# Loads of keys, values and queries of forgetting attention, issued by SyncE instead of GpSimd

## Chip, cores and metric

The kernel runs on one core of a Trainium2 chip. The metric is the device time of one execution in microseconds. The kernel before took 2594.93 us (median of three runs, 2593.69 to 2598.18).

## What is computed

Two layers of an encoder trunk, 2048 tokens of 1024 columns in float32. Each layer normalizes its input, multiplies it by one input projection, hands the columns to three token mixers (a spatial gate, retention, and forgetting attention, "FoX"), multiplies each branch by a gate, concatenates, applies an output projection, normalizes and adds the input. The change touches the third mixer only:

```python
def _forgetting_attention(q, k, v, f_logit):          # 6 heads of 64 columns
    cum_f = jnp.cumsum(jax.nn.log_sigmoid(f_logit), axis=1)
    for i in range(s // Q_BLOCK):
        logits = jnp.einsum('bqhd,bkhd->bhqk', qb, kb) * scale
        logits = logits + cum_f[:, :, q0:q1, None] - cum_f[:, :, None, :q1]
        logits = jnp.where(causal, logits, -jnp.inf)
        p = jax.nn.softmax(logits, axis=-1)
        outs.append(jnp.einsum('bhqk,bkhd->bqhd', p, vb))
```

## The kernel before

Every float32 product is made exact enough by splitting operands into a high part H and a rest L, both of type float32r, and multiplying HH, HL and LH. A layer runs in this order: the input projection, chunk of columns by chunk, with the mixers' other work in the background; then FoX; then the output projection.

During the input projection the split queries and keys of FoX go to DRAM scratch (`qk`, line 241), the split values too (`vscr`, line 290), and the gates (`gscr`, line 329). FoX reads them back head by head. `FoxLoads` keeps a list of loads: `kv(h)` appends the keys in two halves of 512 KB (64 partitions each) and the values of 1024 KB (rows of 512 bytes), into one of four big buffers; `c(h)` appends two loads of the keys' low part with the cumulated gates (`kL`, 264 KB, 66 partitions); `q(u)` appends two loads for a block of 512 queries (256 KB on 128 partitions, 132 KB on 66). `issue()` takes loads from the list and issues them, since line 567 on GpSimd's queue. The scratch is declared float32, the buffers float32r. A layer has 78 such loads, 156 in all.

The first loads are issued during the last chunk of the input projection (lines 497, 501). After that, `fox()` runs one step per value product. A step holds, in the order "ltesv": the low part of the transposed scores on VectorE (L670), a transpose on TensorE (L659) with its copy on ScalarE (L671), an exponential (L646), up to two score tiles (L612, L613 on TensorE, L630 on VectorE), and a value product (L688 with the high part, L689 with the low part). For some key tiles (`ON_POOL`) the split is done on GpSimd instead: ScalarE copies the transposed tile out (`Ts`, L664), and GpSimd writes the high part (L665) and the low part (L666). Behind each step come one `ld.issue()` and one tick of background work. `ld.kv(h + 1)` is called when the first query block of a head (h > 0) ends, `ld.c(h + 1)` when the second ends.

A finished pair of heads (after each query block of an odd head) goes through `finish()`: the gate is loaded (L714, SyncE), the reciprocal of the row sums is transposed and stored to DRAM (L721, SyncE, 4 KB), read back broadcast over partitions in two loads (L724, SyncE), and GpSimd multiplies gate by reciprocal (L726) and the result by the heads' output (L728); SyncE stores it (L730). Fixed numbers of steps lie between these parts.

The order of the work is the order in which the program is written: every engine takes its instructions in that order, and SyncE and GpSimd take their DMA issues in that order too. An engine, or a queue, that waits for one instruction holds all behind it. A DMA on one of the two queues also waits until the DMA eight before it on that queue has landed.

Of the kernel before, what the change touches and what calls it, by code (L numbers as in the profile page):

```python
# [10 lines left out]
F32 = mybir.dt.float32  # L11
# [4 lines left out]
PSUM = bass.MemoryType.PSUM  # L16
# [8 lines left out]
NSB = 4  # L25
EPS = 1e-6
BIG = 1e30
NU = 29  # 4 KB slots for everything of [128, 1024]
NS = 3  # PSUM banks of the scores
# The pace of the work behind the main stream of matrix products, in its steps.  # L30
LEAD = 19  # FoX: score tiles ahead of the value products
SB = 512  # columns of scores that a second score tile in a step may not pass
PRE = 20  # score tiles during the last chunk of the input projection
EMAX = 2  # exponentials that may wait
TK = (1, 4, 7)  # steps of the last projection tile with a transposed tile
ON_POOL = ((3,), (5,), (4, 8), (4, 8, 12))  # key tiles that GpSimd splits, by query block
ORDER = "ltesv"  # of the parts of a step
FX, RA, RB, RC, RD = 2, 2, 4, 1, 3  # between the parts of a finished head pair
QA = 4  # weight row blocks loaded ahead
OL, OE = 9, 16  # normalized tiles behind the output projection, and the last ones  # L40
OW, OD, OP = 22, 3, 4  # output weights: first step, one not used, one split on VectorE
OPRE = 6  # output projection begun before the end of FoX
WU = 30  # matrix products that bring the tensor engine to its full clock


class Background:
    """Work that follows the main stream of matrix products, some ticks behind."""

    def __init__(self):
        self.active = []  # L50
# [26 lines left out]
def trunk(ctx, tc, a, out):  # L77
    nc = tc.nc
# [7 lines left out]
    tp = ctx.enter_context(tc.tile_pool(name="tp", bufs=2))  # L86
    up = ctx.enter_context(tc.tile_pool(name="up", bufs=NU))
    ctx.enter_context(tc.manual_schedule())
# [4 lines left out]

    BANKS = {"S": (512, NS), "B": (512, 6 - NS), "D": (512, 2)}

# [69 lines left out]
                yield  # L165

    def split(src, on_pool=False):
        """The parts H and L of float32 data, H + L exactly the data, each of 12 bits."""
        t = U("HL", F32R)
        n = 1  # L170
        for d in src.shape[1:]:
            n *= d
        H, L = t[:, 0:n], t[:, 512:512 + n]
        v = (lambda ap: ap) if len(src.shape) == 2 else (lambda ap: ap.rearrange("p (k c) -> p k c", c=src.shape[2]))
        nc.scalar.copy(out=v(H), in_=src)  # L175
        eng = nc.gpsimd if on_pool else nc.vector
        eng.tensor_tensor(out=v(L), in0=src, in1=v(H), op=ALU.subtract)  # L177
        return H, L

    def weight_gen(pieces, dst, pool=lambda k: True, ahead=2):  # L180
        """Loads and splits the eight row blocks of a weight chunk, one per step."""
        pend = []
        for k in range(KT + ahead):
            if k < KT:
                if k % 2 == 0:
                    f2 = U("wf")
                f = f2[:, (k % 2) * 512:(k % 2 + 1) * 512]
                off = 0
                for src, w in pieces:
                    ap = src[k]  # L190
                    o_ = f[:, off:off + w]
                    if len(ap.shape) == 3:
                        o_ = o_.rearrange("p (c e) -> p c e", c=ap.shape[1])
                    nc.sync.dma_start(out=o_, in_=ap)
                    off += w
                pend.append(f[:, :off])
            if k >= ahead:
                dst.append(split(pend[k - ahead], on_pool=pool(k)))
            yield
# [5 lines left out]
        return [token_half(hT, t, g) for g in range(2)]  # L205

    def in_proj(l, hT, w0, cur, next_norm):
        """Input projection and everything of it but FoX attention."""
        w_in = a["w_in"][l].rearrange("(k p) e -> k p e", p=P)
        rz = w_in[:, :, 768:2304].rearrange("k p (c e) -> k p c e", c=4)  # L210
        az = w_in[:, :, 0:768].rearrange("k p (c e) -> k p c e", c=3)
        chunks = [("v", [(w_in[:, :, 3072:3456], 384), (w_in[:, :, 3840:3846], 6)]),
                  ("g", [(w_in[:, :, 3456:3840], 384)]),
                  ("q", [(w_in[:, :, 2304:2688], 384)]), ("k", [(w_in[:, :, 2688:3072], 384)])]
# [1 line left out]
        chunks += [(("r", m), [(rz[:, :, :, m * P:(m + 1) * P], 512)]) for m in range(3)]  # L216
        W = [w0] + [[] for _ in chunks[1:]]

        # rows of a head: L, H, ones of the queries; H, L, cumulative forget gates of the keys
        qk = [[dram.tile([2, 2 * HD + 2, SEQ], F32, name=f"qk{l}{w}{m}") for m in range(3)] for w in range(2)]  # L220
        vscr = dram.tile([SEQ, 6, P], F32, name=f"vscr{l}")
        gscr = [dram.tile([P, SEQ], F32, name=f"gscr{l}{m}") for m in range(3)]
# [3 lines left out]
        qbds = tp.tile([P, 2, 2, P], F32, name="qbds", tag="qbds", bufs=1)  # L226
        nc.vector.memset(qbds, 0.0)

        # ---- queries and keys of FoX, transposed: weights stationary, tokens moving
        def qk_post(which, m, b, z):  # L230
            zt = U("zHL", F32R)
            zH, zL = zt[:, 0:512], zt[:, 512:1024]
# [11 lines left out]
        def T_chunks(hs):  # L244
# [5 lines left out]
            for ci in (1, 2, 3):  # L250
                for b in range(4):
                    nxt = []
                    wg = None
                    for m in range(3):
# [4 lines left out]
                        if m == 0 and b == 3:  # L259
                            wg = weight_gen(chunks[ci + 1][1], W[ci + 1], lambda k: k % 3 > 0, QA)  # L260
                            for _ in range(QA):
                                next(wg)
# [17 lines left out]
                    hs = nxt  # L280
            return hs

        # ---- the other chunks: tokens stationary, weights moving
        def v_post(t, z):
            vv = up.tile([P, 6, 2, HD], F32R, name="vv", tag="u")
            zv = heads(z[:, 0:384])
# [184 lines left out]
        for ci in (0, 4, 5, 6, 7, 8):  # L471
# [3 lines left out]
            last = ci == len(chunks) - 1  # L475
            if ci == 4:
                cur = T_chunks(cur)
            for t in range(NT):
# [6 lines left out]
                for k in range(KT):  # L485
                    H, L = cur[k // 4]
# [10 lines left out]
                    if last and k % 4 == 3:  # L497
                        loads.issue()
                    if fx and k % 2 and fx.chunks < PRE and t >= 10:
                        fx.s_step()  # L500
                        loads.issue()
                        fx.e_step()
                    if last and t == NT - 1 and k in TK:
                        fx.l_step()
# [20 lines left out]
    class FoxLoads:  # L525
# [38 lines left out]
        def issue(self, n=1):  # L564
            for _ in range(min(n, len(self.queue))):
                o, i = self.queue.pop(0)
                nc.gpsimd.dma_start(out=o, in_=i)

    class Fox:
        """FoX attention in steps: score steps (one 128 x <=512 tile) run ahead of value steps."""  # L570

        def __init__(self, loads, gscr, y):
            self.ld, self.gscr, self.y = loads, gscr, y
# [74 lines left out]
        def t_step(self):  # L648
# [12 lines left out]
            PH, PL = t[:, 0:512], t[:, 512:1024]  # L661
            if j in ON_POOL[s] and (h, s) != (5, 3):
                Ts = U("Ts")
# [68 lines left out]
    def fox(fx):  # L732
        ld = fx.ld
        for i, (h, s, j) in enumerate(fx.V):
            for op in ORDER:
                if op == "e":
                    fx.e_step()
                    if len(fx.exps) > EMAX:
                        fx.e_step()
                elif op == "l":  # L740
                    fx.l_step()
                elif op == "s":
                    n = 0
                    while n < 2 and fx.si < len(fx.S) and fx.cols < fx.vcols + LEAD * 512 - n * SB:
                        fx.s_step()
# [27 lines left out]
    def out_proj(l, y, W, og, x_src, x_dst, hT, next_w, ahead):  # L773
# [31 lines left out]
                yield from norm(o, pre, hT, t, OL if t < NT - 2 else OE, "B")  # L805

        def last_tile(cur):
            """The last token tile, its first half of columns ahead of the other."""
            t = NT - 1
            x = load_x(x_src(t))  # L810
            o = U("o")
            junk = U("junk")
            ss = small("ss", [P, 2])
            rs = small("rs", [P, 1])
            cs = [slice(g * 512, (g + 1) * 512) for g in range(2)]
            for g in range(2):
                oo = bank("oo", "S")
                for k in range(KT):
                    H, L = cur[k // 4]
                    c = slice((k % 4) * P, (k % 4 + 1) * P)  # L820
                    w = W[2 * k + g]
                    for xx, i, first, last in ((H, 0, True, False), (H, 1, False, False), (L, 0, False, True)):
                        mm(oo, lhsT=xx[:, c], rhs=w[i], start=(k == 0 and first), stop=(k == KT - 1 and last))  # L823
                    bg.tick()
                nc.scalar.activation(out=junk[:, cs[g]], in_=oo, func=AF.Square, accum_out=ss[:, g:g + 1])  # L825
                nc.vector.tensor_tensor(out=o[:, cs[g]], in0=oo, in1=post[:, cs[g]], op=ALU.mult)
            nc.gpsimd.tensor_tensor(out=rs, in0=ss[:, 0:1], in1=ss[:, 1:2], op=ALU.add)  # L827
            nc.gpsimd.tensor_scalar(out=rs, in0=rs, scalar1=1.0 / DM, scalar2=EPS, op0=ALU.mult, op1=ALU.add)  # L828
            nc.gpsimd.tensor_tensor(out=rs, in0=rs, in1=mhalf[:, 0:1], op=ALU.pow)
            for c in cs:  # L830
                nc.vector.scalar_tensor_tensor(out=o[:, c], in0=o[:, c], scalar=rs, in1=x[:, c], op0=ALU.mult, op1=ALU.add)  # L831
                nc.sync.dma_start(out=x_dst(t)[:, c], in_=o[:, c])
# [14 lines left out]
        for t in range(NT):  # L847
# [9 lines left out]
            for k in range(KT):  # L857
                H, L = cur[k // 4]
# [18 lines left out]
        if hT is None:  # L877
            last_tile(cur)
# [26 lines left out]

    wg = weight_gen(first_w(0), W0, lambda k: k % 3 > 0)
    xq[0] = load_x(x_src(0))
    for _ in range(WU):  # the tensor engine at its full clock when the first tile is ready
        nc.tensor.transpose(bank("warm", "B")[:, 0:P], ident, ident)
    pg = load_gain(a["pre_gain"][0])  # L910
    next(wg)
# [2 lines left out]
    first = norm(xq.pop(0), pg, hT, 0, 1, "B", (slice(0, 512), slice(512, DM)))  # L914
# [77 lines left out]
```

## Time and profile before

| | |
|---|---|
| median of three runs | 2594.93 us |
| span of the profiled execution | 2588.5 us |
| TensorE (PE) busy | 2522.0 us, 97% |
| VectorE (DVE) busy | 1663.9 us, 64% |
| ScalarE (ACT) busy | 1258.1 us, 49% |
| GpSimd (POOL) busy | 943.0 us, 36% |
| moved by the hardware-described DMA queue (SyncE's) | 176.61 MB |
| moved by the software-described DMA queue (GpSimd's) | 50.74 MB |

The span runs from the first to the last instruction of the profiled execution; the median of the runs is 6.4 us above it. The profile tells for each instruction when it started, how long it took, and, where its engine sat idle before it, what ended that idle time. A wait is put down to the event that came last. FoX runs from about 749 to 1115 us in the first layer and from about 2030 to 2397 us in the second.

### The profile page before, as it was taken

To read this page: it belongs to the slowest core of one execution; us is meant where nothing else is said; L and a number is where in the kernel's file an instruction comes from. 1 tells how busy PE (TensorE), PEld (TensorE's weight loads), DVE (VectorE), ACT (ScalarE), POOL (GpSimd) and SP (SyncE) were. 2 spreads that over 40 slices of the span, in tenths; PEclk is the share of its full clock that TensorE was granted. 3 is DMA by queue.
4 is the path that set the end of the run, shared out by engine and by line. 5 is a ranking of instruction groups with operands and counts; after the bars stand their busy time and mean duration, and the time that the engine had idled before them with its cause. 6 is when DMAs were issued, how large, how long until landed. Compare 5 with 4: busy or idle time off the path is not lost. (4 is left out here: it accounts for less than half of the span.)

```text
span 2588.5 us, 39556 instructions
## 1 busy us (share of the span) xinstructions
PE 2522.0 (97%) x13112; PEld 2149.4 (83%) x13112; DVE 1663.9 (64%) x4173; ACT 1258.1 (49%) x2967; POOL 943.0 (36%) x1528
## 2 busy tenths in 40 slices
PE   9999999999999999999999999999999999999998
PEld 8888899787888777778898889987878887777887
DVE  5544577666668888854454445666676788878433
ACT  7543433333336788843344444333332478768221
POOL 3111366444443444431120114664344435353200
PEclk9999999999999999999999999999999999989999
DMA  6435411101051556254431354101012415653443
GB/s 212 115 88 121 112 38 37 41 14 37 12 106 39 111 100 130 76 183 134 135 126 69 100 120 101 49 22 38 22 30 42 81 38 128 109 110 97 166 146 114
DMA packets 188428, 229.87 MB, mean 89 GB/s; under 512 B 24640, under 2 KB 130048, under 8 KB 186688
## 3 DMA queue, kind: packets, MB, share of 16 engines
q1 hardware_dynamic: 147712, 176.61, 23.7%
q0 software_dynamic: 40512, 50.74, 10.7%
q8 instruction: 104, 1.70, 0.3%
q14 instruction: 100, 0.82, 0.1%
HBM read 149.20 MB, written 78.09 MB: 88 GB/s over the span
## 5 line engine op out<-in xcount | busy, mean ns | idle before, releaser
L489 PE MATMUL z<-HL 128*128 128x512 f32 (+2 forms) x1536 | 588.5, 383 | 1.8 <-ACT HL L175 1.8
L491 PE MATMUL z<-HL 128*128 128x512 f32 (+2 forms) x1536 | 561.3, 365 | 3.7 <-DVE HL L177 3.6
L490 PE MATMUL z<-HL 128*128 128x512 f32 (+2 forms) x1536 | 559.1, 364 | 0.6 <-POOL HL L177 0.6
L177 DVE TENSOR_TENSOR HL<-hT,HL 128x512 fp32r<-128x512 f32 x576 | 420.7, 779 | 42.1 <-ACT HL L175 33.6
L865 PE MATMUL oo<-HL 128*128 128x512 f32 x1488 | 355.4, 395 | 0.2
L177 POOL TENSOR_TENSOR HL<-wf,HL 128x512 fp32r<-128x512 f32 (+2 forms) x150 | 179.0, 1199 | 451.2 <-ACT HL L175 332.8
L175 ACT CAST HL<-hT 128x512 fp32r<-128x512 f32 x576 | 324.0, 625 | 0.0
L865 PEld LDWEIGHTS oo<-HL 128*128 128x128 f32 x1488 | 273.3, 188 | 57.8 <-DVE HL L177 1.1
L491 PEld LDWEIGHTS z<-HL 128*128 128x128 f32 x1536 | 288.6, 188 | 38.6 <-DVE HL L177 5.3
L489 PEld LDWEIGHTS z<-HL 128*128 128x128 f32 x1536 | 289.7, 189 | 24.6 <-ACT HL L175 3.1
L490 PEld LDWEIGHTS z<-HL 128*128 128x128 f32 x1536 | 290.3, 189 | 22.7 <-POOL HL L177 0.9
L670 DVE TENSOR_TENSOR PHL<-T,PHL 128x512 fp32r<-128x512 f32 (+3 forms) x402 | 241.2, 604 | 16.5 <-ACT PHL L671 15.7
L671 ACT CAST PHL<-T 128x512 fp32r<-128x512 f32 (+3 forms) x402 | 206.0, 519 | 71.0 <-PE T L659 51.7
L267 PE MATMUL z<-HL 128*128 128x512 f32 x576 | 224.4, 390 | 1.0 <-DVE HL L177 1.0
L266 PE MATMUL z<-HL 128*128 128x512 f32 x576 | 224.5, 390 | 0.0
L268 PE MATMUL z<-HL 128*128 128x512 f32 x576 | 224.2, 389 | 0.0
L612 PE MATMUL S<-kv,q 128*128 128x512 f32 (+1 forms) x480 | 214.8, 449 | 2.2 <-DVE mn L630 2.2
L688 PE MATMUL acc<-PHL,kv 128*128 128x512 f32 x480 | 185.2, 386 | 18.6 <-POOL PHL L665 18.6
L348 ACT COPY v<-z 128x128 f32<-128x128 f32 x96 | 25.5, 266 | 353.2 <-DVE w L344 353.0
L689 PE MATMUL acc<-PHL,kv 128*128 128x512 f32 x480 | 180.8, 377 | 6.7 <-POOL PHL L666 5.7
L613 PE MATMUL S<-kL,q 66*128 66x512 f32 (+1 forms) x480 | 178.6, 372 | 0.0
L646 ACT ACTIVATE row<-row,mn 128x1024 f32<-128x1024 f32 (+2 forms) x192 | 158.1, 824 | 35.7 <-DVE mn L630 32.2
(164 smaller groups left out, 4468.8 us busy)
## 6 DMA issues: line engine op xcount, KB each, us to landing
x<-x SPq DMA_DIRECT2D x48, 512.0 KB
qk<-zHL SPq DMA_DIRECT2D x192, 128.0 KB
wf<-w_in SPq DMA_DIRECT2D x96, 192.0 KB
vscr<-vv SPq DMA_DIRECT2D x32, 384.0 KB
wf<-w_in SPq DMA_DIRECT2D x48, 256.0 KB
kv<-qk POOLq DMA_DIRECT2D x24, 512.0 KB, 6.9
kv<-vscr POOLq DMA_DIRECT2D x12, 1024.0 KB, 8.0
q<-qk POOLq DMA_DIRECT2D x48, 256.0 KB, 4.0
```

The costliest lines, as they stand in the source:

```text
L175: nc.scalar.copy(out=v(H), in_=src)
L177: eng.tensor_tensor(out=v(L), in0=src, in1=v(H), op=ALU.subtract)
L266: mm(z, lhsT=wH[:, c], rhs=H, start=(k == 0), stop=False)
L267: mm(z, lhsT=wH[:, c], rhs=L, start=False, stop=False)
L268: mm(z, lhsT=wL[:, c], rhs=H, start=False, stop=(k == KT - 1))
L489: mm(z[:, :n], lhsT=H[:, c], rhs=wH[:, :n], start=(k == 0), stop=False)
L490: mm(z[:, :n], lhsT=H[:, c], rhs=wL[:, :n], start=False, stop=False)
L491: mm(z[:, :n], lhsT=L[:, c], rhs=wH[:, :n], start=False, stop=(k == KT - 1))
L612: mm(S[:, :n], lhsT=Q[0][:, qc], rhs=K[:, kc], start=True, stop=False)
L670: self.low = lambda: nc.vector.tensor_tensor(out=PL[:, c0:], in0=T[:, c0:], in1=PH[:, c0:], op=ALU.subtract)
L671: nc.scalar.copy(out=PH[:, c0:], in_=T[:, c0:])
L865: mm(oo[g], lhsT=x[:, c], rhs=w[g][i], start=(k == 0 and first), stop=(k == KT - 1 and last))
```

## The change

`FoxLoads.issue` issues its loads on SyncE's queue. The destination, a float32r buffer, is named as float32, so that source and destination have the same type and the load is a plain copy of words. What is loaded, into which buffer, and where in the program each load is issued stay as they are. The diff also takes out comments and docstrings, which is left out here.

```diff
         def issue(self, n=1):
             for _ in range(min(n, len(self.queue))):
                 o, i = self.queue.pop(0)
-                nc.gpsimd.dma_start(out=o, in_=i)
+                nc.sync.dma_start(out=o.bitcast(F32), in_=i)
```

## Rows read from the trace of the kernel before

**Rows 1.** The page, its part 1: busy time, share of the span, instructions.

```profile
PE 2522.0 (97%) x13112; PEld 2149.4 (83%) x13112; DVE 1663.9 (64%) x4173; ACT 1258.1 (49%) x2967; POOL 943.0 (36%) x1528
```

**Rows 2.** Waits of TensorE, whole span: us in total, times, longest us.

```profile
PE acc L688 <- POOL PHL L665: 18.6, 8, 3.3
...
PE acc L689 <- POOL PHL L666: 5.7, 8, 0.9
```

**Rows 3.** Windows, one per head's value products: length, busy (instructions), clock, DMA share, GB/s.

```profile
853.85:907.47 53.62, 50.47 (x300) 42.24 (x299) 45.13 (x125) 42.91 (x96) 27.18 (x33) 0.97 0.67 129
...
961.41:1013.36 51.95, 48.93 (x300) 41.17 (x299) 45.23 (x125) 42.84 (x96) 27.24 (x33) 1.00 0.64 133
...
sum 431.77, PE 405.37 PEld 340.05 DVE 358.81 ACT 341.08 POOL 195.00; mean PE 50.67 PEld 42.51 DVE 44.85 ACT 42.63 POOL 24.38
```

**Rows 4.** Timeline of TensorE around 875 us: start, us, instruction, [idle before <- releaser].

```profile
875.66 0.49 PE L688 MATMUL acc<-PHL,kv 128*128 128x512 f32 x1 [2.02 <-POOL PHL L665]
877.01 0.80 PE L689 MATMUL acc<-PHL,kv 128*128 128x512 f32 x1 [0.85 <-POOL PHL L666]
877.60 1.06 PE L659 MATMUL T<-ident,row 128*128 128x128 f32 x4
```

**Rows 5.** Windows of the seven low-clock stretches in FoX, columns as in Rows 3.

```profile
876.80:880.20 3.40, 3.19 (x10) 2.52 (x11) 0.65 (x1) 0.58 (x1) 2.65 (x5) 0.50 0.43 139
...
sum 37.40, PE 33.74 PEld 25.77 DVE 6.83 ACT 6.55 POOL 27.72; mean PE 4.82 PEld 3.68 DVE 0.98 ACT 0.94 POOL 3.96
```

**Rows 6.** Timeline of GpSimd, 857 to 877 us.

```profile
857.37 1.06 POOL L567 DMA_DIRECT2D kv<-qk  x2
...
862.60 1.27 POOL L567 DMA_DIRECT2D kv<-vscr  x1
...
873.74 1.27 POOL L726 TENSOR_TENSOR gy<-gy 128x512 f32<-128x512 f32 x1 [9.32 <-DMA gy<-rd]
875.00 0.61 POOL L665 TENSOR_SCALAR PHL<-Ts 128x512 fp32r<-128x512 f32 x1
875.69 1.26 POOL L666 TENSOR_TENSOR PHL<-Ts,PHL 128x512 fp32r<-128x512 f32 x1
```

**Rows 7.** Timeline of SyncE's queue, 854 to 868 us.

```profile
854.09 0.32 SPq L714 DMA_DIRECT2D gy<-gscr  x1
861.49 0.28 SPq L721 DMA_DIRECT2D rd<-rT  x1
867.05 1.11 SPq L724 DMA_DIRECT2D gy<-rd  x2
```

**Rows 8.** The same of the last head, which has no load beside it.

```profile
1074.63 0.29 SPq L721 DMA_DIRECT2D rd<-rT  x1
1075.86 1.09 SPq L724 DMA_DIRECT2D gy<-rd  x2
```

**Rows 9.** Timeline of GpSimd, same head.

```profile
1079.37 1.28 POOL L726 TENSOR_TENSOR gy<-gy 128x512 f32<-128x512 f32 x1 [3.66 <-DMA gy<-rd]
```

**Rows 10.** Timeline of TensorE: last reader of the buffer of the loads of 857 us.

```profile
851.18 0.34 PE L689 MATMUL acc<-PHL,kv 128*128 128x384 f32 x1
```

**Rows 11.** One window during the loads of the second head, columns as in Rows 3.

```profile
858.00:870.00 12.00, 11.73 (x71) 9.45 (x70) 11.18 (x30) 9.97 (x21) 3.71 (x5) 1.00 1.59 223
```

**Rows 12.** Timeline of SyncE's queue, 911 to 921 us.

```profile
911.86 0.28 SPq L721 DMA_DIRECT2D rd<-rT  x1
919.85 1.09 SPq L724 DMA_DIRECT2D gy<-rd  x2
```

**Rows 13.** Timeline of GpSimd, 925 to 929 us.

```profile
925.75 1.29 POOL L726 TENSOR_TENSOR gy<-gy 128x512 f32<-128x512 f32 x1 [7.80 <-DMA gy<-rd]
927.11 1.27 POOL L728 TENSOR_TENSOR gy<-o,gy 128x512 f32<-128x512 f32 x1
928.33 0.59 POOL L567 DMA_DIRECT2D kL<-qk  x1
```

**Rows 14.** Timeline of TensorE: end of the second stall, first use of that kL.

```profile
929.62 0.50 PE L688 MATMUL acc<-PHL,kv 128*128 128x512 f32 x1 [2.70 <-POOL PHL L665]
...
935.83 0.28 PE L613 MATMUL S<-kL,q 66*128 66x128 f32 x1
```

**Rows 15.** Window over the whole span, line 567 alone: POOL's time in it.

```profile
0.00:2588.50 2588.50, 98.04 (x156) 0.99 0.35 89
```

**Rows 16.** The gate's load on SyncE's queue: issue ns min/median/max, first to last.

```profile
L714 SPq DMA_DIRECT2D gy<-gscr x24: 319/424/1057, 854.1 to 2398.0; - x24
```

## Prediction

> **What bounds the kernel now.** I read the page's busy shares first: TensorE works 97% of the span, so only time in which TensorE stands still or runs slowly can be won, and whatever GpSimd or the queues spend beside it costs nothing by itself [rows 1]. So the next view is TensorE's own waits. No wait of TensorE on a DMA is among them; the largest in FoX are on GpSimd: 18.6 us in eight waits for the high part (L665) and 5.7 us in eight for the low part (L666) that follow directly, 24.3 us together [rows 2]. The eight lie in the four middle heads of each layer. Cut FoX at each head's first value product, and these eight heads take 431.77 us [rows 3].
>
> The third view is the first stall on three engines. TensorE waits 2.02 us before L688 and 0.85 us before L689, and the transposes after them take 1.06 us [rows 4], because the clock has fallen: from 876.8 us the granted clock is 0.50, the lower level of 1.2 GHz, for 3.4 us. There are seven such stretches in FoX, 37.40 us with TensorE busy for 33.74 us of it, and each begins at one of the eight stalls [rows 5]. One stall (head 961.41:1013.36) kept a clock of 1.00; that head took 51.95 us, while its neighbour with a fall took 53.62 us [rows 3].
>
> Why GpSimd is late: it had the high part waiting, but L726 stands ahead of it in GpSimd's order, and L726 was held 9.32 us for the broadcast reciprocals (DMA gy<-rd) [rows 6]. Those come from a chain on SyncE: L721 issued at 861.49, L724 not before 867.05, because it needs the landing of L721's 4 KB, and L726 starts at 873.74 [rows 6, 7]. In the last head, which has no loads beside it, the same chain goes 1074.63, 1075.86, 1079.37: 4.74 us instead of 12.25 [rows 8, 9]. What lies beside the slow one are 2 MB of keys and values that GpSimd issued at 857.37 to 862.60 [rows 6]. So TensorE's stalls come from loads that fly at the wrong moment, together with GpSimd's fixed order.
>
> **The change, part by part.** *GpSimd loses 156 issues*, 98.04 us of its time [rows 15]. On TensorE's path lies only what stood between L726 and L665 in a stall: the kL issue of 0.59 us in the pattern of the second stall [rows 13]. GpSimd is otherwise idle 64% of the span [rows 1], so I take nothing for the rest; the cover is that idle time.
>
> *SyncE gains 156 issues.* The nearest rows are its own loads of 256 KB: 0.32 to 1.06 us, median 0.42 [rows 16], so 50 to 165 us of a queue that in FoX issues a DMA only every few microseconds [rows 7, 12]. For the values load, with its many 512-byte rows, GpSimd's 1.27 us [rows 6] is the nearest; I take 0.4 to 1.3 us. This costs nothing unless one of SyncE's own steps gets late, which comes next.
>
> *The loads move in time.* On GpSimd they stood behind its arithmetic: the buffers of the loads from 857.37 us were free when L689 ended at 851.52 (851.18 + 0.34) [rows 6, 10]. SyncE has nothing to do before L714 at 854.09 [rows 7]. So the query pair and the first half of the keys go out from about 851.6, the gate at 854.1, the second half and the values right behind it, 3 to 7 us earlier than now. Ahead of L721 that makes 388 + 512 + 256 + 512 + 1024 = 2692 KB, 2.76 MB. At the 223 GB/s of the loads now [rows 11] that takes 12.4 us, and if data moves from about 853 it is through at 865.4. L721 would land between 862.7 (the 1.23 us of the quiet chain [rows 8]) and about 866. The kL load, which now flies beside L724, then stands behind it, so L724 to L726 takes the quiet 3.51 us [rows 8, 9]: L726 starts between 866.2 and 869.5 instead of 873.74.
>
> How early is early enough? Without a stall TensorE wants the high part at 873.64 (875.66 - 2.02) and the low part a quarter of a microsecond later [rows 4]. L726, L665 and L666 take 1.27, 0.61 and 1.26 us [rows 6], 3.2 us in a row with their gaps, so L726 has to start by 870.6. It does, with 1.1 to 4.4 us to spare.
>
> *The second pattern* (stalls two and four of a layer): L721 goes out at 911.86 and L724 only at 919.85, L726 at 925.75, then L728 and a kL issue ahead of the high part [rows 12, 13]. In the program only the query pair stands ahead of L721, and one half of the keys ahead of L724. On SyncE L721 lands after 1.2 to 2.6 us, L724 goes out by 914.5, behind 512 KB (2.4 us at 223 GB/s), and L726 starts near 920 at the latest. TensorE wants the high part at 926.92 (929.62 - 2.70) [rows 14]; L726, L728, L665 and L666 take 4.5 us, so 922.7 is enough. Two to four microseconds are left.
>
> *Are the loads ever late?* Those behind L721 and L724 now wait on SyncE. The tightest use now is the kL issued at 928.33 and read at 935.83 [rows 13, 14]; it stands behind two values and keys loads, not behind arithmetic, and goes out ten microseconds earlier. The second half of the keys waits for L724's issue, which even at its present 919.85 [rows 12] leaves 15 us to the next head's first score, near that 935.83. I take nothing for it.
>
> *The sum.* Idle removed: 18.6 + 5.7 = 24.3 us. Clock: in 37.40 us TensorE worked 33.74 us at half speed, which is 16.9 us of work at full speed, so 16.9 us come back if the clock falls with the stalls. Together 41.2 us: 39.0 us if one stall in twenty remains. Against the span 2588.5 gives 2547.3 to 2549.5; with the 6.4 us by which the median stands above the span, 2553.7 to 2555.9. I say 2555.
>
> *What is late next.* VectorE: 44.85 us of work in a mean head of 54.0 us [rows 3], in a head of 48.8 us then 92%. In the low-clock stretches it worked only 6.83 of 37.40 us [rows 5], so it has no backlog and starves as soon as TensorE slows; I take it as not binding, with up to 10 us lost as the upper end of the likeliest case.
>
> **Two rules against it.** The trace shows the issuing order to matter: 9.32 us of held GpSimd, 98 us of issues [rows 6, 15]. The Trainium skill, "DMA: Bandwidth & Descriptors", section "Issuing engines are not separate DMA queues", says that all issuers share the same 16 DMA engines and that the choice only saves the sequencer's time, usually small. By that rule the time would stay near 2595; it is the third case below, worked out from rows there.
> The trace shows a 4 KB store slowed from 1.23 to 5.56 us beside loads of another queue [rows 7, 8]. The same page, "Queues, rings and completion order", says that a DMA engine takes turns between queues but consumes one ring in order, so on one queue the store would wait for all that stands ahead. That is the second and the fourth case; no row here shows loads and store on one queue.
>
> **Rivals.** (a) Half the stalls stay: 2.76 MB ahead of L721 drain later than I think, and the first pattern (four of the eight) keeps its waits, while the second pattern, with little ahead of L721, is cured. For it speaks the margin of 1.1 us at its short end. Half of 41.2 us: 2574.
> (b) No change: L726 still waits about as long, since loads and chain share the DMA engines whoever issues, and only the issues between L726 and L665 go, 0.59 us in four stalls: 2.4 us, 2592.5. Against it: the quiet chain, and buffers that are free 6 us before the loads go out.
> (c) Slower: the small store and the broadcast stand behind the loads on one queue, and the queue drains slowly. It decides in the first pattern, where L726 starts later than now if the 2.76 MB need more than about 17 us from 853, below 162 GB/s. At 107 GB/s, half the rate of rows 11, they end at 878.8, L726 starts near 882.5, 8.8 us later than now: four times 8.8 is 35 us more, less the 20.6 us of the other pattern, so 2609. The rate of 223 GB/s speaks against it.
>
> **How the numbers follow.** The full cure 0.70 (2546 to 2564), half of it 0.15 (2574, to 2582), no change 0.08, slower 0.07. The range from 2545 to 2579 holds the first and most of the second. About 0.2%, 5 us, is what a measurement tells from no change: faster 0.86, same 0.07, slower 0.07.
>
> **What would show it.** Right: TensorE's waits on L665 and L666 nearly gone; the clock at 1.00 through FoX; middle heads of about 49 us; L721 to L726 under 9 us; key loads out before L714. Wrong at the timing step: loads early, but L721 landing as late as now. Wrong at the clock step: waits gone and low-clock stretches still there. Wrong at the last step: waits on VectorE in the place of those on GpSimd.

## The result, and the profile after

The changed kernel takes 2548.74 us (median of four runs, 2546.40 to 2550.55) against 2594.31 us for the kernel before (four runs, 2589.82 to 2598.18): a ratio of 0.9834, 95% interval 0.9818 to 0.985. That is 45.6 us faster; the prediction was 2555 us, its likeliest case. The profiled execution has a span of 2546.9 us, 41.6 us shorter than that of before.

Part 1 of the page, to be laid beside [rows 1]:

```profile
PE 2503.3 (98%) x13112; PEld 2138.8 (84%) x13112; DVE 1663.4 (65%) x4173; ACT 1257.4 (49%) x2967; POOL 851.3 (33%) x1372
```

GpSimd has 156 instructions and 91.7 us less. TensorE has the same 13112 matmuls and 18.7 us less busy time: it does the same work faster, so the clock must have changed, and the windows below show it. Its waits (us in total, times, longest), beside [rows 2]:

```profile
PE sc L458 <- POOL vu L451: 6.8, 8, 1.1
...
PE acc L689 <- POOL PHL L666: 0.3, 1, 0.3
```

The 18.6 us on L665 have no row any more, and of the 5.7 us on L666 one wait of 0.3 us is left. Nothing new has come in their place. The same eight heads as in [rows 3], with the same columns (the third number from the end is the granted clock):

```profile
2215.11:2264.44 49.33, 48.71 (x300) 41.12 (x299) 45.11 (x125) 42.89 (x96) 19.41 (x20) 1.00 0.53 136
...
sum 388.47, PE 386.14 PEld 329.17 DVE 357.94 ACT 340.35 POOL 135.44; mean PE 48.27 PEld 41.15 DVE 44.74 ACT 42.54 POOL 16.93
```

The granted clock is 1.00, the upper level of 2.4 GHz, in all eight. They take 388.47 us instead of 431.77: 43.3 us less, of which TensorE's busy time makes 19.2 us (405.37 to 386.14) and its idle time the other 24.1 us. That is the whole gain of the span (the rest of it is 1.7 us longer). The slowest head, 49.33 us, is the one with the wait of 0.3 us.

Now the chain that made GpSimd late. First SyncE's queue, then GpSimd, in the first pattern, beside [rows 6, 7]; this execution runs about 0.75 us later here (L721 at 862.24 instead of 861.49):

```profile
852.30 0.75 SPq L567 DMA_DIRECT2D q<-qk  x2
853.10 0.45 SPq L567 DMA_DIRECT2D kv<-qk  x1
854.79 0.32 SPq L714 DMA_DIRECT2D gy<-gscr  x1
855.15 0.45 SPq L567 DMA_DIRECT2D kv<-qk  x1
855.65 0.59 SPq L567 DMA_DIRECT2D kv<-vscr  x1
862.24 0.29 SPq L721 DMA_DIRECT2D rd<-rT  x1
866.86 1.09 SPq L724 DMA_DIRECT2D gy<-rd  x2
```

```profile
870.64 1.30 POOL L726 TENSOR_TENSOR gy<-gy 128x512 f32<-128x512 f32 x1 [7.25 <-DMA gy<-rd]
```

The loads are out by 856.2 instead of 863.9 (862.60 + 1.27 [rows 6]). L721 still takes 4.62 us to land, against 5.56 before and 1.23 in the quiet head [rows 8]; what has become short is L724 to L726, 3.78 us instead of 6.69. From L721 to L726 the chain takes 8.40 us, before 12.25. GpSimd still waits 7.25 us for it, but TensorE no longer waits for GpSimd here. The same two engines in the second pattern, beside [rows 12, 13]:

```profile
907.73 0.28 SPq L721 DMA_DIRECT2D rd<-rT  x1
908.05 0.49 SPq L567 DMA_DIRECT2D kv<-qk  x1
909.12 1.09 SPq L724 DMA_DIRECT2D gy<-rd  x2
910.25 0.59 SPq L567 DMA_DIRECT2D kv<-qk  x1
910.89 0.59 SPq L567 DMA_DIRECT2D kv<-vscr  x1
911.58 5.55 SPq L567 DMA_DIRECT2D kL<-qk  x1
```

```profile
915.39 1.28 POOL L726 TENSOR_TENSOR gy<-gy 128x512 f32<-128x512 f32 x1 [2.79 <-DMA gy<-rd]
...
920.27 0.62 POOL L665 TENSOR_SCALAR PHL<-Ts 128x512 fp32r<-128x512 f32 x1 [2.24 <-ACT Ts L664]
```

L721 has landed after 1.39 us, L726 starts 7.66 us after L721 instead of 13.89, and GpSimd reaches L665 before its input is there: it waits for ScalarE, as it should. One row is new: the issue of kL takes 5.55 us, where the issues around it take half a microsecond. SyncE itself is held there, behind 2 MB of keys and values.

The wait of 0.3 us that is left belongs to a first pattern too, in the third of the four middle heads of the second layer (SyncE's queue, GpSimd, TensorE):

```profile
2222.76 0.76 SPq L721 DMA_DIRECT2D rd<-rT  x1
2228.41 1.09 SPq L724 DMA_DIRECT2D gy<-rd  x2
```

```profile
2232.19 1.28 POOL L726 TENSOR_TENSOR gy<-gy 128x512 f32<-128x512 f32 x1 [8.27 <-ACT Ts L664]
```

```profile
2235.49 0.50 PE L689 MATMUL acc<-PHL,kv 128*128 128x512 f32 x1 [0.35 <-POOL PHL L666]
```

The store takes 5.65 us here and the chain 9.43, and TensorE waits 0.35 us before L689.

### The profile page after: what moved, and what is told of

Its sections match the earlier page's. It is cut to its first block, busy times and chain, and to the rows that moved or that the text cites. A ratio compares the mean times of both kernels' runs of the same rounds, so it can differ in the third digit from the quotient of the medians.

```text
span 2546.9 us, 39524 instructions
## 1 busy us (share of the span) xinstructions
PE 2503.3 (98%) x13112; PEld 2138.8 (84%) x13112; DVE 1663.4 (65%) x4173; ACT 1257.4 (49%) x2967; POOL 851.3 (33%) x1372
## 5 line engine op out<-in xcount | busy, mean ns | idle before, releaser
L489 PEld LDWEIGHTS z<-HL 128*128 128x128 f32 x1536 | 289.8, 189 | 24.1 <-ACT HL L175 2.7
L670 DVE TENSOR_TENSOR PHL<-T,PHL 128x512 fp32r<-128x512 f32 (+3 forms) x402 | 241.4, 604 | 17.5 <-ACT PHL L671 17.4
L688 PE MATMUL acc<-PHL,kv 128*128 128x512 f32 x480 | 181.1, 377 | 0.2 <-ACT PHL L671 0.2
L689 PE MATMUL acc<-PHL,kv 128*128 128x512 f32 x480 | 176.5, 368 | 1.5 <-DVE PHL L670 1.0
L646 ACT ACTIVATE row<-row,mn 128x1024 f32<-128x1024 f32 (+2 forms) x192 | 158.2, 824 | 35.8 <-DVE mn L630 35.8
```

What stands on the lines that cost most here:

```text
L489: mm(z[:, :n], lhsT=H[:, c], rhs=wH[:, :n], start=(k == 0), stop=False)
L670: self.low = lambda: nc.vector.tensor_tensor(out=PL[:, c0:], in0=T[:, c0:], in1=PH[:, c0:], op=ALU.subtract)
```

## Experiments

The theory ("chain"): what counts is when the 2 MB of keys and values fly, seen from the store L721 and the broadcast L724. The rivals: GpSimd's 98 us of issue time were the gain; or the gain is one of the queue, whatever the time. Each pair of times below is from one chip; the runs of before on the three chips had medians of 2594.30 (fifteen runs), 2596.12 (seven) and 2593.95 us (nine).

**Only keys and values on SyncE.** Of the 156 loads, 36 move; queries and kL stay on GpSimd. (Five lines are added, so L670, L726, L729 and L731 here are L665, L721, L724 and L726 elsewhere; the entries of the keys and values carry a third item.)

```diff
-                o, i = self.queue.pop(0)
-                nc.gpsimd.dma_start(out=o, in_=i)
+                x = self.queue.pop(0)
+                if len(x) > 2:
+                    nc.sync.dma_start(out=x[0].bitcast(F32), in_=x[1])
+                else:
+                    nc.gpsimd.dma_start(out=x[0], in_=x[1])
```

> Only the 36 loads of keys and values go to SyncE; the 120 loads of queries and low key parts stay on GpSimd. Chain theory (the stalls come from keys and values that fly beside the small store L721 and the broadcast L724): nearly all of the gain, 2549 to 2558 us, no TensorE waits on L665 over 2 us in total. GpSimd-time theory (the gain is the 98 us that GpSimd no longer spends on issues): keys and values are 26 us of the 98, so about a quarter of the gain, near 2583 us.

Measured: 2554.42 us (2551.07 to 2556.24), ratio 0.9854 (0.9825 to 0.9882). No wait of TensorE on GpSimd's two parts is left. SyncE's queue and GpSimd in the first pattern:

```profile
861.00 0.29 SPq L726 DMA_DIRECT2D rd<-rT  x1
866.45 1.09 SPq L729 DMA_DIRECT2D gy<-rd  x2
```

```profile
870.02 1.28 POOL L731 TENSOR_TENSOR gy<-gy 128x512 f32<-128x512 f32 x1 [7.34 <-DMA gy<-rd]
```

The store takes 5.45 us, the chain 9.02 us, and that is short enough. Three quarters of the issues are still on GpSimd, and nearly the whole gain is there: GpSimd's time was not what it came from. Whether the 5.7 us between this median and that of the full change are real is not settled: the intervals of the two ratios overlap, but the runs also lie mostly above those of the third experiment on the same chip (2547.18 to 2552.49 us). What there is of them does not lie in the chain: the eight middle heads take 387.90 us in this profiled execution, 388.47 in that of the kernel after.

**Only queries and kL on SyncE.** The same edit with `if len(x) == 2`, so that the keys and values stay on GpSimd, at their old times.

> The other part alone: queries and low key parts on SyncE, keys and values on GpSimd as before. Chain theory: most of the stalls stay, 2575 to 2592 us, with L721 still landing 4 us or more after its issue in the first pattern. GpSimd-time theory: three quarters of the gain, near 2560 us.

Measured: 2575.85 us (six runs, 2561.16 to 2579.13), ratio 0.9921 (0.9894 to 0.9947). TensorE keeps seven waits on L665's line, 12.7 us, and seven on L666's, 5.4 us. SyncE's queue, GpSimd and TensorE in the first pattern:

```profile
861.52 0.28 SPq L726 DMA_DIRECT2D rd<-rT  x1
863.83 1.11 SPq L729 DMA_DIRECT2D gy<-rd  x2
```

```profile
862.63 1.25 POOL L572 DMA_DIRECT2D kv<-vscr  x1
872.45 1.28 POOL L731 TENSOR_TENSOR gy<-gy 128x512 f32<-128x512 f32 x1 [8.57 <-DMA gy<-rd]
```

```profile
874.38 0.50 PE L693 MATMUL acc<-PHL,kv 128*128 128x512 f32 x1 [0.69 <-POOL PHL L670]
```

Here the store was quick (2.31 us; the expected 4 us or more in this pattern did not come), and still L726's product starts 10.93 us after it: now the broadcast, issued right behind the 1 MB of values, takes 8.62 us. So the loads delay whichever of the two small transfers flies beside them. The stalls are shorter than before, and only three of the seven are followed by a fall of the clock (6.8, 6.8 and 3.4 us at 0.50); that, and the shorter stalls, is the part of the gain that this half of the change brings.

**All on GpSimd, keys and values earlier.** The kernel before, but the keys and values of head h+2 go out at the end of head h.

```diff
-            if s == 0 and j == 3 and h > 0:
-                ld.kv(h + 1)
+            if s == 3 and j == 15:
+                ld.kv(h + 2)
+                ld.issue(len(ld.queue))
```

> All loads stay on GpSimd, but a head's keys and values are issued together at the end of the head before, some four steps earlier in the program. Chain theory: the first pattern is cured, the second (where they now fly just ahead of L721) at least in part: 2550 to 2575 us with GpSimd issuing and its 98 us of issues unchanged. Queue theory (one hardware-described queue serves the small DMAs faster than two queues do, whenever the loads leave): the stalls stay, 2585 us or more. GpSimd-time theory: no change, 2594 us.

Measured: 2549.00 us (2547.18 to 2552.49), ratio 0.9832 (0.9808 to 0.9857); the middle heads take 48.4 to 48.8 us, and TensorE has no wait on L665 or L666. SyncE's queue and GpSimd:

```profile
862.25 0.28 SPq L721 DMA_DIRECT2D rd<-rT  x1
864.30 1.11 SPq L724 DMA_DIRECT2D gy<-rd  x2
```

```profile
850.80 1.22 POOL L567 DMA_DIRECT2D kv<-vscr  x1
...
868.61 1.28 POOL L726 TENSOR_TENSOR gy<-gy 128x512 f32<-128x512 f32 x1 [4.69 <-DMA gy<-rd]
```

The values go out at 850.80, twelve microseconds before they did [rows 6], and the chain takes 6.36 us. In the second pattern, where they now fly ahead of L721, it takes 10.11 us, and TensorE does not wait there either. The gain is that of the change, with every load still issued by GpSimd. The time of the loads is the cause; neither the issuer nor the queue is.

**All on SyncE, keys and values between store and broadcast.** The kernel after, with the keys and values issued between L721 and L724.

```diff
             nc.sync.dma_start(out=scr, in_=rT)
+            if s in (0, 3):
+                self.ld.kv(h + 1 if s == 0 else h + 2)
+                self.ld.issue(len(self.ld.queue))
...
-            if s == 0 and j == 3 and h > 0:
-                ld.kv(h + 1)
```

> All loads on SyncE as in the kernel after, but keys and values are issued between the store L721 and the broadcast L724, in both patterns. Chain theory: L724 stands behind 2 MB, 7 to 9 us at 223 to 300 GB/s, L726 starts 11 us or more after L721, the stalls and the low clock come back: 2570 to 2600 us. Queue theory and GpSimd-time theory: as fast as the kernel after, 2549 us.

Measured: 2593.01 us (ten runs, 2587.87 to 2595.61), ratio 0.9999 (0.9984 to 1.0014): the whole gain is lost with every load on SyncE. TensorE's waits, SyncE's queue, GpSimd and TensorE (lines three higher from 722 on, so L727 is the broadcast and L729 the product):

```profile
PE acc L688 <- POOL PHL L665: 19.7, 8, 3.4
...
PE acc L689 <- POOL PHL L666: 5.6, 8, 0.9
```

```profile
861.92 0.29 SPq L721 DMA_DIRECT2D rd<-rT  x1
862.26 1.09 SPq L567 DMA_DIRECT2D kv<-qk  x2
863.40 0.59 SPq L567 DMA_DIRECT2D kv<-vscr  x1
864.08 6.02 SPq L727 DMA_DIRECT2D gy<-rd  x2
```

```profile
875.59 1.26 POOL L729 TENSOR_TENSOR gy<-gy 128x512 f32<-128x512 f32 x1 [12.51 <-ACT rows L646]
```

```profile
877.50 0.80 PE L688 MATMUL acc<-PHL,kv 128*128 128x512 f32 x1 [3.39 <-POOL PHL L665]
```

The store has landed after 2.16 us, but the two broadcast issues take 6.02 us (6.76 in the second pattern), and the data another 5.5 us: 13.67 us of chain. Five of the eight stalls come with a fall of the clock to 0.50, for 3.4 or 6.8 us. GpSimd's idle time is put down to L646 here, which is the profile's guess for a wait for several things; the product needs the broadcast.

**No broadcast at all.** The kernel before, without L724; the product takes the gate twice.

```diff
-            for i in range(2):
-                nc.sync.dma_start(out=rb[i * HD:(i + 1) * HD], in_=scr[4 * i:4 * i + 4].rearrange("r p -> (r p)").partition_broadcast(HD))
...
-            nc.gpsimd.tensor_tensor(out=g, in0=g, in1=rb, op=ALU.mult)
+            nc.gpsimd.tensor_tensor(out=g, in0=g, in1=g, op=ALU.mult)
```

> The kernel before, all loads on GpSimd where they were, without the two loads L724 that read the reciprocals back: L726 multiplies the gate by itself, so the output is not normalized, and GpSimd has nothing to wait for there. Chain theory: the eight stalls vanish without moving a load, 2549 to 2556 us, clock 1.00 through FoX. GpSimd-time theory and queue theory: the stalls stay, near 2590 us.

Measured: 2544.78 us (2543.28 to 2545.25), ratio 0.981 (0.9783 to 0.9837). GpSimd (L724 is the product here):

```profile
862.33 1.27 POOL L567 DMA_DIRECT2D kv<-vscr  x1
...
864.16 1.05 POOL L724 TENSOR_TENSOR gy<-gy 128x512 f32<-128x512 f32 x1
870.75 0.61 POOL L665 TENSOR_SCALAR PHL<-Ts 128x512 fp32r<-128x512 f32 x1 [5.53 <-ACT Ts L664]
```

The loads go out at their old times and hurt nobody once GpSimd does not wait for the broadcast: TensorE has no wait on L665 or L666 left, and the clock does not fall in FoX. This shows the link from the loads to TensorE, and it is about the floor of what this chain could give (the 48 loads of the broadcast, 128 KB each, are gone too): the change is within about 4 us of it.

**GpSimd kept busy.** The kernel after, with an idle instruction of GpSimd at each of the 156 issues (the line that declares `idle` is left out).

```diff
                 o, i = self.queue.pop(0)
                 nc.sync.dma_start(out=o.bitcast(F32), in_=i)
+                nc.gpsimd.tensor_scalar(out=idle, in0=causal, scalar1=1.0, scalar2=0.0, op0=ALU.mult, op1=ALU.add)
```

> The kernel after with an idle GpSimd instruction of about 0.6 us (a scale of 128x512 numbers that nobody reads) at each of the 156 places where a load is issued, so that GpSimd has its 98 us back. Chain theory: no change to speak of, 2548 to 2553 us. GpSimd-time theory: most of the loss returns, 2580 to 2594 us.

Measured: 2548.10 us (2546.42 to 2551.68), ratio 0.9824 (0.98 to 0.9848). Part 1 of its page:

```profile
PE 2501.1 (98%) x13112; PEld 2138.7 (84%) x13112; DVE 1661.1 (65%) x4173; ACT 1257.8 (49%) x2967; POOL 945.5 (37%) x1528
```

GpSimd has its 156 instructions back, in number and in time [rows 1], and the gain is whole. Its 98 us were worth nothing.

**All on SyncE, keys and values earlier,** beside the kernel after on the same chip. The edit of the third experiment, in the kernel after.

> The kernel after, all loads on SyncE, but the keys and values of head h+2 are put on the list and issued at once at the end of head h, not from the fourth key tile of the next head on. Chain theory (the time at which the 2 MB fly beside store and broadcast is what counts): the store L721 of the first pattern lands in under 3 us instead of 4.61, the product L726 of that pattern starts 2 us or more earlier than 870.64, the small waits of TensorE on L665 and L666 that are left in the kernel after (0.35 us at the largest) are gone; since these were nearly nothing, the time is 2544 to 2549 us, at most 4 us below the kernel after. Rival (one ring in order on SyncE: whatever is issued there early holds the queue for what follows): the gate load L714 and the store come later by the 5 us that SyncE's issues were seen to be held behind 2 MB, TensorE waits again, 2555 us or more.

> The kernel after, unaltered, on the same chip as the run beside it, to compare the two directly. Both theories: 2546 to 2551 us, as before.

Measured: 2547.41 us (2545.30 to 2547.98), ratio 0.9815 (0.98 to 0.983), against 2547.64 us (2546.90 to 2548.68), ratio 0.9818 (0.9803 to 0.9832), for the kernel after. There is no difference to be seen. The two patterns with the earlier loads, SyncE's queue and then GpSimd:

```profile
861.79 0.28 SPq L721 DMA_DIRECT2D rd<-rT  x1
863.01 1.09 SPq L724 DMA_DIRECT2D gy<-rd  x2
...
901.49 5.04 SPq L714 DMA_DIRECT2D gy<-gscr  x1
...
907.53 0.28 SPq L721 DMA_DIRECT2D rd<-rT  x1
913.05 1.09 SPq L724 DMA_DIRECT2D gy<-rd  x2
```

```profile
866.51 1.29 POOL L726 TENSOR_TENSOR gy<-gy 128x512 f32<-128x512 f32 x1 [3.56 <-DMA gy<-rd]
...
916.70 1.29 POOL L726 TENSOR_TENSOR gy<-gy 128x512 f32<-128x512 f32 x1 [4.57 <-DVE PHL L670]
```

Both theories saw a part: in the first pattern the chain is as short as in the quiet head (4.72 us; the store lands after 1.22), and in the second the gate load is held 5.04 us behind the loads, the store lands after 5.52, and the chain takes 9.17 us. TensorE has time enough for both, so nothing is gained or lost. The repeated kernel after shows how near the edge it is (SyncE's queue, GpSimd, TensorE):

```profile
861.31 1.68 SPq L721 DMA_DIRECT2D rd<-rT  x1
867.21 1.09 SPq L724 DMA_DIRECT2D gy<-rd  x2
```

```profile
871.55 1.29 POOL L726 TENSOR_TENSOR gy<-gy 128x512 f32<-128x512 f32 x1 [9.09 <-ACT rT L719]
```

```profile
874.84 0.51 PE L689 MATMUL acc<-PHL,kv 128*128 128x512 f32 x1 [0.86 <-POOL PHL L666]
```

**All first patterns side by side.** From the rows above, L721 to L724, L724 to L726, and what TensorE then waits before L688, in us:

| kernel | store | broadcast | chain | wait at L688 |
|---|---|---|---|---|
| quiet last head, before | 1.23 | 3.51 | 4.74 | |
| after, loads earlier | 1.22 | 3.50 | 4.72 | 0 |
| before, loads earlier | 2.05 | 4.31 | 6.36 | 0 |
| after | 4.62 | 3.78 | 8.40 | 0 |
| only keys and values moved | 5.45 | 3.57 | 9.02 | 0 |
| after, third middle head of layer two | 5.65 | 3.78 | 9.43 | 0 (0.35 at L689) |
| after, again | 5.90 | 4.34 | 10.24 | 0 (0.86 at L689) |
| only queries and kL moved | 2.31 | 8.62 | 10.93 | 0.69 |
| before | 5.56 | 6.69 | 12.25 | 2.02 |
| loads behind the store | 2.16 | 11.51 | 13.67 | 3.39 |

In the last three rows the chain less the wait is 10.24, 10.23 and 10.28 us. The table takes one head of a run, or two, but of eight runs, with the loads on either queue; the other first patterns of those last three kernels that make TensorE wait before L688, eight of them, give 10.10 to 10.27 us. One number explains the column: TensorE stands still before L688 for what the chain takes beyond 10.2 us. Before L689 it does so already from about 9.1 us (9.43 - 0.35; another head of the repeated kernel after gives 9.45 - 0.36; in the row of 10.24 us L688 itself came slightly late, so the 0.86 us tell a little less).

## Why the prediction was right, point by point

**The bound and the chain** were right. TensorE's waits on L665 and L666 were the time to win; GpSimd's issues were not (the kept-busy GpSimd); the loads beside store and broadcast were the cause (loads earlier on GpSimd: the gain; loads late on SyncE: none; no broadcast: the gain).

**The move in time** came as told: query pair and first half of the keys ahead of the gate, the second half and the values right behind it, at 852.30, 853.10, 854.79, 855.15 and 855.65, which is 851.6 and 854.1 after the shift of 0.75 us.

**The landing of the store** came at its late end. With the same shift L724 is issued at 866.11, where the upper end was 866, and L726 starts at 869.89, where it was 869.5. It sufficed because the deadline was right: the prediction's 870.6 is 9.1 us after L721, and the runs give 9.1 too. But of the 1.1 to 4.4 us to spare little was there. The four first patterns of the profiled execution take 8.40, 8.34, 8.22 and 9.43 us: three are 0.7 to 0.9 us early, and the last is late, against the prediction's own sign of "under 9 us". Two of the four in the repeated run are late (10.24 and 9.45 us). What they cost TensorE is 0.35 to 0.86 us each. That was the margin on which rival (a) rested, and it came nearer than its 0.15 says; that the pattern was cured so fully is in part luck.

**The second pattern**: L724 after 1.39 us (told: at most 2.6), L726 7.66 us after L721 (told: at most 8.1, needed by 10.8). Right, with 3.2 us to spare.

**The issues on SyncE** were mis-sized at one end. The 156 take 92.7 us together (told 50 to 165), the values load 0.59 us (told 0.4 to 1.3), and most others 0.3 to 0.5; but the longest takes 5.55 us, against the bound of 1.06. It cost nothing, because what stood behind it was kL, and the rows of the last experiments show that it could have been the gate or the broadcast. The kL of [rows 13], the first of its pair, is that very issue: it starts 3.85 us after L721 and ends 9.40 us after it, where it started 16.47 us after it before. That is 12.6 us earlier by its start (told ten), 7.7 by its end (before 17.06); TensorE did not wait for it.

**The sum.** Idle time removed: told 24.3, found 24.1 us in the eight heads. Clock: told 16.9, found 19.2 us; the clock falls vanished with the stalls. Together 43.3 us in the heads, 41.6 in the span, told 41.2; the span of 2546.9 lies 0.4 us under the range of 2547.3 to 2549.5. VectorE works 44.74 of 48.56 us in a mean head and has not become the bound.

**The term that was wrong** is the 6.4 us that the prediction put around the span. In all executions recorded since, of either kernel, the device time is 1.7 to 1.9 us above the span (after: 2548.63 to 2546.9). By that the other 4.6 us was the spread of the kernel before, of which the profiled execution was a short one: its fifteen runs on one chip go from 2583.72 to 2601.25 us with mean granted clocks of 0.994 to 0.987, the short ones at the high clock. The kernel after has hardly a stall to vary with: 2546.40 to 2550.55 us at 0.998 or 0.999. Set 1.8 us in that term's place, and the same steps give 2549 to 2551 instead of 2554 to 2556.

**A slip in rival (c)**: it calls 107 GB/s half of 223. Half is 111.5, by which the loads end at 877.7, L726 starts near 881.2, 7.5 us later than before the change, and the case comes to about 2604 us instead of 2609. Nothing else hung on it.

**The two rules.** Moved on GpSimd alone, the loads gave the same gain (ratio 0.9832 against 0.9834). The change of issuer was worth 45.6 us only because it changed when an engine that works in order got to the issue. The Trainium skill, "DMA: Bandwidth & Descriptors", section "Issuing engines are not separate DMA queues", says that all issuers share the same DMA engines. To that the trace agrees: the 1 MB of values on GpSimd's queue slowed SyncE's broadcast from 3.51 to 8.62 us.

On one queue the store landed after 4.62 us behind 2.7 MB; beside the loads of another queue it had taken 5.56. The Trainium skill, "DMA: Bandwidth & Descriptors", section "Queues, rings and completion order", says that a DMA engine consumes one ring in order. The 4.62 us fit that, but no run here tells it apart from the sharing of the engines alone.

## What to carry to other kernels

When a fixed order makes an engine wait for a small transfer, look at which large transfers fly beside it, and price a move of the large ones by the time at which they would go out, on whichever queue. A plain change of order on the old queue can be worth as much as the new queue; and on the new queue the wrong order loses everything. If the kernel has stalls that make the clock fall, add no distance between one profiled span and the median to the new kernel: part of it is the spread that the change removes.

## What the runs showed that was not expected

An issue of SyncE itself, normally 0.3 to 0.6 us, took 5.55 us (kL, kernel after) and 5.04 us (gate, loads earlier), and two broadcast issues together 6.02 and 6.76 us (loads behind the store). In six of the profiled runs SyncE issues the values, 72 loads in all, and these tell when it happens. What SyncE issues right behind the values (0.1 us after their issue ends) takes 3.2 to 6.2 us, in all 34 cases, whatever it moves. Four loads of queries 2.6 us behind take 2.5 to 3.2 us. What comes 4.8 us behind or later, in the other 34 cases, takes 0.3 to 1.7 us; L721 in the first pattern of the kernel after, 6.0 us behind, is one of them. So the hold ends some 3 to 6 us after the values are issued. Why SyncE is held, and whether by the many 512-byte rows of the values or by all that is under way with them, is not settled.

Not every stall of TensorE makes the clock fall: of the seven stalls with only queries and kL moved, three are followed by 3.4 or 6.8 us at the lower level of 1.2 GHz, while the 0.69 us stall at 874.38 left the granted clock at 1.00 for the next 50 us.
